# A hybrid decoder step on one core: when the decode branch's cached values are loaded, and in which buffers

## The chip, the core and the metric

The kernel runs as one program on one core of a Trainium2 chip. The metric is the device time of one execution in microseconds (us), as the median of several runs. Five engines work side by side, each through its own list of instructions in the order in which the program was recorded: PE (matmuls; PEld are its weight loads), DVE, ACT, POOL, and SP, which here only issues transfers (DMAs). An engine that waits for another holds up everything behind it on its own list.

## What is computed

Two layers of a decoder. Each layer handles 512 prompt tokens and 64 sample tokens (8 sequences of 8 tokens) with shared weights. The part that the change touches is the attention of the sample tokens over a cache of old keys and values, three head groups with window and dilation (128, 1), (512, 4) and (2048, 16):

```python
def dilated_group(q, k_all, v_all, q_idx, window, dilation):
    n_keys = window // dilation + 1
    idx = q_idx[:, None] - jnp.arange(n_keys)[None, :] * dilation
    ...
    s = jnp.einsum('bthd,btjhd->bhtj', q, kg).astype(jnp.float32) * (HEAD_DIM ** -0.5)
    ...
    m = jnp.max(s, axis=-1, keepdims=True)
    p = jnp.exp(s - m)
    den = jnp.sum(p, axis=-1, keepdims=True)
    o = jnp.einsum('bhtj,btjhd->bthd', p / den, vg.astype(jnp.float32))

def layer(x, ...):
    proj = rmsnorm(x, norm1) @ w_in            # q, k, v, u, ga, gb
    ...
    mixed = jax.nn.sigmoid(ga) * (o_a @ w_pa) + jax.nn.sigmoid(gb) * (o_b @ w_pb)
    x = x + mixed @ w_o
    x = x + jnp.square(jax.nn.relu(rmsnorm(x, norm2) @ w_up)) @ w_down
```

## The kernel before

**Stages of a layer.** PE first does the q, k, v projections in units ("d", "a", "b", "e", "c"), for two passes `p` of two heads each. Then follow the four products for `u` (weights `wu`), the gate products for branch b (`wgb`, `wpb`), those for branch a (`wga`, `wpa`), the output product (`wo`) and the feed-forward part. The prompt's attention (`prompt`) and the sample's attention (`decode`) run beside these as generators. A small planner keeps a model time per engine, and each generator yields until a moment of it or until a mark such as `("O", p)`. So the order on every engine is fixed when the program is recorded.

**The decode branch.** `decode(p, qb)` has two parts. In the first, DVE and POOL multiply nine key chunks by the queries `qb` and fold them into scores `SC`. In the second, PE multiplies the weights by nine value chunks into the PSUM tile `po`. A chunk is a tile of 128 x 8 x 128 floats, 512 KB, loaded by `chunk` on SP's queue: the 128 and 512 groups in one DMA, the 2048 group in two DMAs of half the size. All chunks live in four buffers with the tag `kc`. In the value part one chunk of the 128 group comes first, and then four steps `c`, each with a chunk of the 512 group and one of the 2048 group. After each step DVE copies the result from `po` to `at`, and PE begins the next step only after that copy. Before, four value chunks (128, 512/0, 2048/0, 512/1) are asked for together ahead of the softmax; each of the other five is asked for when a buffer has been read: the first at the mark `N`, the others through `more()` after each chunk of a step.

**The queries' tile.** `qb` holds 128 x 8 x 3 x 128 floats, filled by eight DMAs from the DRAM copy `DQ`. It has one buffer, for both passes of a layer. After the new keys' products of a pass it is read no more, and after the second pass it is not filled again in that layer.

**What stands on SP's queue near the end of the first pass.** `out_p<-nat` writes keys and values of the prompt from `nat`. After the projections the memory of `nat` is given to the tiles of the `u` stage, so DVE's first write into a `u` tile waits for these two writes. The first of them waits on SP until `DV<-nat` (issued by ACT in `turn`) has landed, because the two share one of the eight completion counters of SP's and ACT's queues. `sn` (the pooling state) stands behind them.

**Where PE is alone with decode.** At the first gate product of branch a, the main sequence stops at `until("D", 1)`: there the value part of the second pass runs on PE with no other product beside it.

Of the kernel before, what the change touches and what calls it, by code (L numbers as in the profile page):

```python
# [7 lines left out]
F32 = mybir.dt.float32  # L8
# [83 lines left out]
def hybrid_decoder_kernel(ctx: ExitStack, tc: tile.TileContext, a, o):  # L92
# [21 lines left out]
    def C(name):  # L114
        lo, hi = OFF[name]
        return const[:, lo:hi]
# [127 lines left out]
    def side(gen, delay=0.0):  # L244
        sides.append([now[0] + delay if not isinstance(delay, tuple) else delay, gen])

    def mark(*key, lat=0.0):
        ev[key] = now[0] + lat
# [137 lines left out]
    def after(*lanes, lag=0.2):  # L386
        return "at", max([now[0]] + [x.t for x in lanes]) + lag
# [158 lines left out]
    for l in range(L):  # L546
# [7 lines left out]
        dp = kvn = ve1 = None  # L554
# [307 lines left out]
        def decode_q(p, DN):  # L862
            rope(DN[:, 0:6].rearrange("p n (h d) -> p (n h) d", h=2).unsqueeze(1), *rope_d, 64, 1, 12)
            yield 1.6
            DQ = drp.tile([64, 384], F32, tag=f"dq{l}{p}", name="DQ")
            Q.dma_start(DQ, DN[:, 0:3].rearrange("p n f -> p (n f)"))
            yield 2.6
            if p == 1:
                yield ("K", 0)
            qb = dp.tile([128, 8, 3, 128], F32, tag="qb", name="qb", bufs=1)  # L870
            for b in range(8):
                Q.dma_start(qb[16 * b:16 * b + 16].rearrange("p t n f -> p (t n f)"),
                            DQ[8 * b:8 * b + 8].rearrange("t e -> (t e)").unsqueeze(0).to_broadcast([16, 3072]))
            side(decode(p, qb))
# [24 lines left out]

        def chunk(p, n, c, s):  # L900
            src = a["c" + n][l].rearrange("b r (s f) -> b r s f", s=2)[:, :, s, 128 * p:128 * p + 128]
            t = dp.tile([128, 8, 128], F32, tag="kc", name="kc", bufs=4)
            if n == "128":
                Q.dma_start(t, src.rearrange("b (g i) f -> (b g) i f", g=16))
            elif n == "512":
                Q.dma_start(t, src.rearrange("b (g i c) f -> (b g) i c f", g=16, c=4)[:, :, c])
            else:
                for i in range(2):
                    Q.dma_start(t[:, 4 * i:4 * i + 4],
                                src.rearrange("b (g i c) f -> (b g) i c f", g=16, c=16)[:, :, c + 4 * i])  # L910
            return t

        def decode(p, qb):
            todo = [("512", 0), ("2048", 0)] + [(n, c) for c in range(1, 4) for n in ("512", "2048")]
            if p == 1:
                yield ("V", 0)
            k1 = chunk(p, "128", 0, 0)
            got = [chunk(p, *todo.pop(0), 0)]
            if p == 1:
                yield ("D", 0)  # L920
            SC = dp.tile([128, 23, 8, 2], F32, tag="SC", name="SC", bufs=1)
            sq = SC.rearrange("p s t h -> p s (t h)")
            got += [chunk(p, *todo.pop(0), 0) for _ in range(2)]
            late = []

# [37 lines left out]
            sm = tp.tile([128, 3, 16], F32, tag="dsm", name="dsm", bufs=1)  # L963
            V.tensor_reduce(out=sm[:, 0], in_=sq.rearrange("p s q -> p q s"), axis=AX.X, op=ALU.max)
            todo = [("128", 0)] + [(n, c) for c in range(4) for n in ("512", "2048")]
            got = [chunk(p, *x, 1) for x in todo[:4]]
            del todo[:4]
            yield ("O", p)
            yield after(V)
            po = opp.tile([128, 512], F32, tag="o", name="po")  # L970
# [17 lines left out]
            V.tensor_mul(sq, sq, sm[:, 2].unsqueeze(1).to_broadcast([128, 23, 16]))  # L988
            yield after(V)

            def spread(s0, n, t):
                src = sq[:, s0:s0 + n] if t is None else SC[:, s0:s0 + n, t]
                q = 16 if t is None else 2
                return (src.unsqueeze(2).to_broadcast([128, n, 8, q]),
                        C("bd8").unsqueeze(1).unsqueeze(3).to_broadcast([128, n, 8, q]))

            for s0, n, vv in ((20, 3, kvn[:, 3:6]), (0, 8, got.pop(0))):
                pb = dp.tile([128, 8, 8, 16], F32, tag="prod", name="pb", bufs=3)
                V.tensor_mul(pb[:, 0:n], *spread(s0, n, None))
                yield after(V)  # L1000
                for s in range(n):
                    T.matmul(pof, vv[:, s], pb[:, s].rearrange("p b q -> p (b q)"), start=(s0 == 20 and s == 0),
                             stop=False, skip_group_check=True)
            mark("N", p)
            got.append(chunk(p, *todo.pop(0), 1))

            def more():
                if todo:
                    got.append(chunk(p, *todo.pop(0), 1))

            def pairs(c):
                pb = dp.tile([128, 8, 2, 8, 2], F32, tag="prod", name="pb2", bufs=3)
                qs = dp.tile([128, 8, 16, 2], F32, tag="pb3", name="pb3", bufs=2)
                for i in range(2):
                    t = c + 4 * i
                    V.tensor_mul(pb[:, :, i], *spread(8, 8, t))
                    V.tensor_mul(qs[:, 4 * i:4 * i + 4], SC[:, 16:20, t].unsqueeze(2).to_broadcast([128, 4, 16, 2]),
                                 C("bdz")[:, 8 - 8 * i:24 - 8 * i].unsqueeze(1).unsqueeze(3)
                                 .to_broadcast([128, 4, 16, 2]))
                return [pb[:, s].rearrange("p i b h -> p (i b h)") for s in range(8)], \  # L1020
                       [qs[:, s].rearrange("p x h -> p (x h)") for s in range(8)]
# [4 lines left out]
            for c in range(4):  # L1026
                area = po_[:, 128 + 128 * (c % 3):256 + 128 * (c % 3)]
                ws = nxt
                if c < 3:
                    nxt = pairs(c + 1)  # L1030
                for w, vv in zip(ws, (got.pop(0), got.pop(0))):
                    for s in range(8):
                        r = 32 * (s % 4)
                        T.matmul(area[r:r + 32], w[s], vv[:, s], start=False, stop=(w is ws[1] and s > 3),
                                 skip_group_check=True)
                        if s % 4 == 3:
                            yield 0.1
                    more()
                if c == 2:
                    mark("V", p)  # L1040
                V.tensor_copy(at[:, c], area)
                if c == 0:
                    V.memset(area, 0.0)
# [160 lines left out]
        for f in range(8):  # L1204
# [9 lines left out]
            t = gate.pop(0)  # L1214
# [411 lines left out]
```

## Time and profile before

| what | value |
|---|---|
| median of 3 runs | 1742.92 us (1741.65 to 1745.79) |
| the profiled execution, its own time | 1745.91 us |
| its span from first to last instruction | 1744.1 us |
| PE busy in it | 1638.9 us, 94% |
| DVE, ACT, POOL busy | 67%, 40%, 14% |
| mean granted TensorE clock | 0.96 of 2.4 GHz |

The page gives the busy time of each engine, the share of the granted clock by slices, and the waits. A granted clock of 0.50 is the lower of the two levels, 1.2 GHz. PE is busy nearly all the time, so the few stretches where it stands still, and those where it runs at the lower level, are where time can go.

### The profile page before, as it was taken

What the parts mean: (1) busy time and instruction counts of PE and PEld (TensorE: products, weight loads), DVE (VectorE), ACT (ScalarE), POOL (GpSimd) and SP (SyncE); (2) the same over time, 40 slices, a digit from 0 to 9 for tenths busy, and PEclk for the clock granted to TensorE, in tenths of its full rate; (3) what the DMA queues carried; (4) which work ended last, traced back from release to release, by engine and by line L of the source; (5) the groups of instructions that cost most, each with busy time, mean ns of one, the idle gap of its engine ahead of it and who ended that gap; (6) DMA issues with size and microseconds to landing.
All of it is one profiled execution on the core that took longest, in us unless ns stands there. A gap on an engine that the chain in (4) does not pass through costs nothing.

```text
span 1744.1 us, 30710 instructions
## 1 busy us (share of the span) xinstructions
PE 1638.9 (94%) x12608; PEld 1592.0 (91%) x12608; DVE 1166.7 (67%) x1892; ACT 695.4 (40%) x1210; POOL 239.6 (14%) x370
## 2 busy tenths in 40 slices
PE   8999879899989999999999989797998999999997
PEld 8989769889889999999998988696998999999996
DVE  5489569646766666666636966794566666766664
ACT  5544332123444343443434544221344433443444
POOL 0041023000011111111001400330000211111102
PEclk9999989989989999999999999898998999999999
DMA  4665643434235545543428475335251455445431
GB/s 174 129 205 136 171 117 109 141 92 137 100 112 192 179 165 187 192 159 103 133 81 184 144 184 152 112 100 142 78 187 44 161 176 193 171 167 176 160 100 62
DMA packets 140166, 248.93 MB, mean 143 GB/s; under 512 B 10332, under 2 KB 100956, under 8 KB 137706
## 3 DMA queue, kind: packets, MB, share of 16 engines
q1 hardware_dynamic: 132398, 187.65, 35.7%
q0 software_dynamic: 4736, 56.34, 9.1%
q10 hardware_dynamic: 2892, 2.98, 0.5%
q8 instruction: 99, 1.62, 0.4%
q14 instruction: 41, 0.34, 0.1%
HBM read 233.10 MB, written 68.58 MB: 173 GB/s over the span
## 4 chain that ended last, share of the span: by engine, by line
PE 76%; DVE 10%; DMA 6%; ACT 4%; issue 2%; SPq 0%; POOL 0%; DVEq 0%; POOLq 0%; ACTq 0%
PE mm L380 41%; PE pa L380 10%; PE mmq L380 10%; PE pc L380 5%; DMA kc<-in_c 2%; PE pb L380 2%; DVE wl L357 2%; PE po L380 2%; PE psd L380 2%; DMA DV<-nat 1%; ACT wh L357 1%; PE O L380 1%; DVE SC L357 1%; PE trx L384 1%; DVE xr L357 1%
## 5 line engine op out<-in xcount | busy, mean ns | idle before, releaser
L380 PE MATMUL mm<-m,wh 128*128 128x256 f32 (+1 forms) x2560 | 450.4, 296 | 3.4 <-DVE xr L357 2.1
L380 PEld LDWEIGHTS mm<-m,wh 128*128 128x128 f32 x2560 | 386.7, 189 | 4.4 <-ACT wh L357 1.7
L380 PE MATMUL mm<-m,wl 128*128 128x320 f32 (+1 forms) x1280 | 281.7, 297 | 8.0 <-DVE wl L357 8.0
L357 DVE TENSOR_TENSOR wl<-raw,wh 128x1024 fp32r<-128x1024 f32 (+2 forms) x195 | 220.8, 1134 | 77.1 <-ACT wh L357 73.5
L357 ACT CAST wh<-rawu 128x512 fp32r<-128x512 f32 (+1 forms) x158 | 123.1, 783 | 350.6 <-DVE rawu L357 299.9
L357 ACT CAST wh<-raw 128x1024 fp32r<-128x1024 f32 (+2 forms) x195 | 183.1, 940 | 171.2 <-PE mm L380 86.0
L380 PE MATMUL mm<-a,wh 128*128 128x256 f32 (+1 forms) x1280 | 231.4, 304 | 12.7 <-DVE ud L357 12.4
L380 PEld LDWEIGHTS mm<-m,wl 128*128 128x128 f32 x1280 | 217.6, 190 | 8.9 <-DVE wl L357 8.9
L380 PE MATMUL mmq<-wh,a 128*128 128x256 f32 x1152 | 219.0, 290 | 1.2 <-DVE a L357 0.5
L380 PEld LDWEIGHTS mm<-a,wh 128*128 128x128 f32 x1280 | 194.9, 193 | 17.0 <-issue 16.3
L380 PEld LDWEIGHTS mmq<-wh,a 128*128 128x128 f32 x1152 | 182.6, 195 | 4.3 <-issue 1.4
L357 DVE TENSOR_TENSOR xr<-xr,mm 128x576 f32<-128x576 f32 (+2 forms) x152 | 108.7, 716 | 116.0 <-PE mm L380 110.8
L357 DVE TENSOR_TENSOR wl<-rawu,wh 128x512 fp32r<-128x512 f32 (+1 forms) x158 | 140.2, 889 | 65.6 <-ACT wh L357 61.9
L380 PE MATMUL pa<-h,wh 128*128 128x288 f32 x896 | 181.7, 295 | 0.0
L357 POOL COPY pace<-beat 1x1 f32<-1x1 f32 x112 | 60.7, 542 | 867.9 <-DVE beat L357 867.9
L380 PE MATMUL mmq<-wl,a 128*128 128x256 f32 x576 | 164.8, 286 | 0.0
L380 PEld LDWEIGHTS pa<-h,wh 128*128 128x128 f32 x896 | 144.8, 188 | 0.0
L380 PE MATMUL mm<-a,wl 128*128 128x256 f32 (+1 forms) x640 | 138.7, 299 | 0.0
L380 PE MATMUL pa<-h,wl 128*128 128x288 f32 x448 | 132.4, 296 | 0.0
L380 PEld LDWEIGHTS mmq<-wl,a 128*128 128x128 f32 x576 | 112.0, 194 | 0.0
L380 PEld LDWEIGHTS mm<-a,wl 128*128 128x128 f32 x640 | 109.5, 192 | 0.0
L380 PE MATMUL pc<-h,wh 128*128 128x288 f32 x512 | 104.6, 296 | 0.0
(212 smaller groups left out, 2581.8 us busy)
## 6 DMA issues: line engine op xcount, KB each, us to landing
out_s<-in_c POOLq DMA_DIRECT2D x64, 508.0 KB, 5.0
rawu<-in_wup SPq DMA_DIRECT2D x60, 512.0 KB
raw<-in_wd SPq DMA_DIRECT2D x60, 512.0 KB
kc<-in_c SPq DMA_DIRECT2D x40, 512.0 KB
raw<-in_wq SPq DMA_DIRECT2D x35, 512.0 KB
kc<-in_c SPq DMA_DIRECT2D x64, 256.0 KB
out_s<-in_c POOLq DMA_DIRECT2D x32, 504.0 KB, 5.1
raw<-in_wgb SPq DMA_DIRECT2D x16, 512.0 KB
```

The lines of the kernel that those rows point to most:

```text
L357: return op(*args, **kw)
L380: return self.eng.matmul(out, w, x, **kw)
L384: return self.eng.transpose(out, x, one)
```

## The change

`values()` now issues the value loads as a generator of its own. The 128 chunk is still asked for at once. In the first pass (`p == 0`) the next three follow 8 us of planner time later and 3 us apart. In the second pass (`p == 1`) six more follow 0.3 us apart, the last three of them into three parts of a tile with the tag `qb`, the buffer that the queries of that pass held. The value part waits for the mark `("values", p)`, so that all of them have been recorded; `more()` asks for the rest. In the second pass that leaves two chunks (512/3 and 2048/3).

```diff
         def chunk(p, n, c, s):
             src = a["c" + n][l].rearrange("b r (s f) -> b r s f", s=2)[:, :, s, 128 * p:128 * p + 128]
-            t = dp.tile([128, 8, 128], F32, tag="kc", name="kc", bufs=4)
+            if room:
+                t = room.pop(0)
+            else:
+                t = dp.tile([128, 8, 128], F32, tag="kc", name="kc", bufs=4)
...
+        room = []
...
             todo = [("128", 0)] + [(n, c) for c in range(4) for n in ("512", "2048")]
-            got = [chunk(p, *x, 1) for x in todo[:4]]
-            del todo[:4]
+            got = [chunk(p, *todo.pop(0), 1)]
+
+            def values():
+                for i in range(3 if p == 0 else 6):
+                    if i == 3:
+                        more = dp.tile([128, 3, 8, 128], F32, tag="qb", name="kc", bufs=1)
+                        room.extend(more[:, j] for j in range(3))
+                    got.append(chunk(p, *todo.pop(0), 1))
+                    yield (3.0, 0.3)[p]
+                mark("values", p)
+
+            side(values(), 8.0 if p == 0 else 0.3)
             yield ("O", p)
...
+            yield ("values", p)
             for s0, n, vv in ((20, 3, kvn[:, 3:6]), (0, 8, got.pop(0))):
...
             mark("N", p)
-            got.append(chunk(p, *todo.pop(0), 1))
-
-            def more():
-                if todo:
-                    got.append(chunk(p, *todo.pop(0), 1))
+            more()
```

The lists of PE, DVE, ACT and POOL are the same before and after, apart from line numbers and buffer names. Only SP's list changes, at two places in each layer.

The first place is SP's list at the end of the first pass; `wgb` is the first gate weight, `kc` are value chunks (the two DMAs of a 2048 chunk are the rows of 128x4x128).

```order
-L340 DMA kc<-in_c 128x8x128 x2
-L340 DMA kc<-in_c 128x4x128 x2
-L340 DMA kc<-in_c 128x8x128
-L340 DMA qb<-DQ 16x3072 x8
-L340 DMA raw<-in_wgb 128x1024
-L340 DMA out_p<-nat 128x4x128 x2
+L340 DMA kc<-in_c 128x8x128
+L340 DMA qb<-DQ 16x3072 x8
+L340 DMA raw<-in_wgb 128x1024
+L340 DMA kc<-in_c 128x8x128
+L340 DMA out_p<-nat 128x4x128 x2
+L340 DMA kc<-in_c 128x4x128 x2
```

Ahead of the two `out_p` writes stood four chunks, and now two; the chunks 2048/0 and 512/1 follow behind them, ahead of `sn`.

The second place is SP's list in the second pass, after the first four value chunks.

```order
 L340 DMA raw<-in_wpa 128x256
-L340 DMA raw<-in_wga 128x1024
-L340 DMA kc<-in_c 128x4x128 x2
-L340 DMA kc<-in_c 128x8x128
-L340 DMA kc<-in_c 128x4x128 x2
+L340 DMA kc<-in_c 128x4x128 x2
+L340 DMA kc<-in_c 128x8x128
+L340 DMA kc<-in_c 128x4x128 x2
+L340 DMA raw<-in_wga 128x1024
 L340 DMA kc<-in_c 128x8x128
 L340 DMA kc<-in_c 128x4x128 x2
```

The weight load `wga` moved behind the five DMAs of 2048/1, 512/2 and 2048/2. Those five no longer wait for a read of a `kc` buffer by PE, since they go into the queries' tile; the last three DMAs (512/3, 2048/3) still do.

## Rows read from the trace of the kernel before

**Rows 1.** The page: its head and section 1 (busy us and share).

```profile
span 1744.1 us, 30710 instructions
PE 1638.9 (94%) x12608; PEld 1592.0 (91%) x12608; DVE 1166.7 (67%) x1892; ACT 695.4 (40%) x1210; POOL 239.6 (14%) x370
```

**Rows 2.** Timeline, PE: start us, us, engine line op [idle before <-releaser].

```profile
188.47 1.30 PE L380 MATMUL mm<-a,wh 128*128 128x256 f32 x4 [5.91 <-DVE ud L357]
...
1046.32 1.30 PE L380 MATMUL mm<-a,wh 128*128 128x256 f32 x4 [6.45 <-DVE ud L357]
```

**Rows 3.** Timeline, DVE, the first write of a u tile in layer 0.

```profile
187.50 0.69 DVE L357 TENSOR_TENSOR u<-mm,rb 128x512 f32<-128x512 f32 x1 [8.53 <-DMA out_p<-nat]
```

**Rows 4.** Timeline, SP's issues (start us, us), layer 0, then one of layer 1.

```profile
167.40 9.38 SPq L340 DMA_DIRECT2D qb<-DQ  x8
...
183.81 0.95 SPq L340 DMA_DIRECT2D out_p<-nat  x2
187.50 0.37 SPq L340 DMA_DIRECT2D sn<-in_state_pool  x1
...
1041.65 0.95 SPq L340 DMA_DIRECT2D out_p<-nat  x2
```

**Rows 5.** Timeline, ACT's issues of DV, layer 0 and layer 1.

```profile
173.46 0.37 ACTq L340 DMA_DIRECT2D DV<-nat  x1
...
1030.77 0.38 ACTq L340 DMA_DIRECT2D DV<-nat  x1
```

**Rows 6.** Waits of SP from 170 to 200 us: us in total, times, longest.

```profile
SPq L340 <- DMA DV<-nat: 5.8, 1, 5.8
```

**Rows 7.** Windows: stretch, us, busy by engine, PEclk, DMA share, GB/s.

```profile
160.00:165.00 5.00, 5.00 (x48) 4.75 (x47) 3.56 (x10) 1.15 (x6) 0.00 (x0) 1.00 0.81 233
165.00:170.00 5.00, 5.00 (x47) 4.44 (x45) 4.62 (x9) 4.95 (x16) 0.00 (x0) 1.00 1.05 282
```

**Rows 8.** Timeline, PE, value part of the second pass, layer 0.

```profile
345.62 0.43 PE L380 MATMUL po<-kc,pb 128*32 128x128 f32 x8 [0.48 <-DMA kc<-in_c]
347.70 0.66 PE L380 MATMUL po<-kc,pb 128*32 128x128 f32 x8 [1.66 <-DMA kc<-in_c]
349.58 1.51 PE L380 MATMUL po<-kc,pb 128*32 128x128 f32 x24 [1.22 <-DVE pb L357]
351.29 0.65 PE L380 MATMUL po<-kc,pb 128*32 128x128 f32 x8 [0.21 <-DMA kc<-in_c]
353.19 2.24 PE L380 MATMUL po<-kc,pb 128*32 128x128 f32 x32 [1.24 <-DMA kc<-in_c]
355.85 1.91 PE L380 MATMUL po<-const,at 128*128 128x32 f32 x8 [0.41 <-DVE at L357]
```

**Rows 9.** Waits of PE from 1190 to 1240 us, layer 1's value part.

```profile
PE po L380 <- DMA kc<-in_c: 5.9, 6, 2.2
```

**Rows 10.** Timeline, PE, value part of the second pass, layer 1.

```profile
1199.45 1.35 PE L380 MATMUL po<-kc,pb 128*32 128x128 f32 x32
...
1206.44 1.45 PE L380 MATMUL po<-kc,pb 128*32 128x128 f32 x24 [2.23 <-DMA kc<-in_c]
...
1210.05 1.50 PE L380 MATMUL po<-kc,pb 128*32 128x128 f32 x24 [1.25 <-DMA kc<-in_c]
```

**Rows 11.** Windows: after the stop of layer 0; the value part of layer 1.

```profile
188.40:193.10 4.70, 4.63 (x19) 4.67 (x20) 3.52 (x9) 2.38 (x4) 0.00 (x0) 0.50 0.44 131
...
1206.90:1215.20 8.30, 5.39 (x64) 3.22 (x57) 0.58 (x2) 0.00 (x0) 0.00 (x0) 0.50 0.45 113
```

**Rows 12.** Timeline, SP's issues in the second pass, layer 0.

```profile
333.71 0.34 SPq L340 DMA_DIRECT2D raw<-in_wga  x1
342.30 7.82 SPq L340 DMA_DIRECT2D kc<-in_c  x8
```

**Rows 13.** Timeline, layer 0: ACT's cast of that wga, and PE's first read of sn.

```profile
363.03 1.04 ACT L357 CAST wh<-raw 128x1024 fp32r<-128x1024 f32 x1
...
197.70 0.61 PE L384 MATMUL trs<-const,sn 120*128 120x120 f32 x4
```

More of the change, by code (lines that the diff above doesn't have):

```diff
@@ L989, in decode, with more @@
             yield after(V)
+            def more():
+                if todo:
+                    got.append(chunk(p, *todo.pop(0), 1))
             def spread(s0, n, t):
```

## Prediction

> **What bounds the kernel now.** I read the page's head first: PE is busy for 1638.9 of 1744.1 us [rows 1]. The change leaves the lists of PE, DVE, ACT and POOL as they are, so it can win only where PE stands still, or runs at the lower clock, because of something on SP's queue. The waits of PE by stretches show two such places per layer, and the timeline shows each one's chain.
>
> The first place is the start of the `u` stage. PE stands for 5.91 us in layer 0 and 6.45 us in layer 1 [rows 2]. DVE is named there, but DVE itself stood for 8.53 us until the `out_p` writes had landed, since the `u` tiles take over the memory of `nat` [rows 3]. These writes were issued at 183.81 [rows 4], after SP had waited 5.8 us for `DV<-nat` [rows 6], which ACT had issued at 173.46 [rows 5]. So DV took 10.35 us to land, and in layer 1 10.88 us (1030.77 to 1041.65) [rows 4, 5]. In that time SP's queue was still moving what had been issued earlier: four value chunks and eight `qb` loads, whose issues alone lasted 9.38 us from 167.40 [rows 4].
>
> The second place is the value part of the second pass, where PE has no other product to do. In layer 0 it waits before five groups of matmuls [rows 8]; in layer 1 six waits for chunks make 5.9 us [rows 9]. The eight DMAs for the last five chunks are issued only from 342.30 on, as the buffers are read [rows 12].
>
> **Part 1, first pass, loads spaced out.** In SP's list the chunks 2048/0 and 512/1 move from ahead of `qb` and `out_p` to behind them, and 512/0 to behind `qb`. Two chunks of 512 KB, 1.05 MB, are then no longer ahead of DV and `out_p`. While the chunks moved, the DMAs carried 233 and 282 GB/s [rows 7]. That makes 4.5 us or 3.7 us; I take 3.7, from the stretch in which the last chunks moved. If DV waits for what stands ahead of it, it lands 3.7 us sooner, `out_p` is issued at 180.1 in place of 183.81, and DVE's write follows by as much. PE's stops shrink from 5.91 to 2.2 and from 6.45 to 2.75 us: 7.4 us in the two layers. Something of the stop stays, because DV still has the eight `qb` loads ahead of it.
>
> The bounds: at the least nothing, if DV's time doesn't depend on those chunks; at the most the whole stop, 12.4 us. The clock comes on top. After the stop of layer 0 PE ran 4.70 us at 0.50, 1.2 GHz [rows 11], so it lost half of that, 2.35 us. A stop of 2 to 3 us may end in the same stretch or in none, so I count nothing in the sum and 2 x 2.35 us in the range; the other way, a shorter stop might let the lower clock fall on PE's work in place of its idle time, and I allow the same 2.35 us per layer as a loss.
>
> The Trainium skill, page "DMA: Bandwidth & Descriptors", section "Queues, rings and completion order", speaks against this part: an engine "round-robins between the queue rows it has work for", so a transfer on ACT's queue shares the engines with SP's queue and doesn't stand behind it. By that rule the sum of part 1 would be nothing, and the time is that of the second rival below. The trace agrees only in part: sharing equally, DV's 512 KB with as much from SP's queue would need 3.7 to 4.5 us at the rates of [rows 7], and it took 10.35 and 10.88 [rows 4, 5].
>
> What moves to behind `out_p` must still be in time. `sn` gets three more DMAs ahead of it; PE reads it at 197.70 [rows 13], 10.2 us after its issue at 187.50 [rows 4], and both move by the same amount. PE reads the value chunks of the first pass behind that in its list. The two chunks ahead of `sn` are 1.05 MB, 4.5 us at 233 GB/s [rows 7], and fit into the 10.2. If that cover were gone, PE would wait one for one.
>
> **Part 2, second pass, seven of nine chunks ahead.** The chunks 2048/1, 512/2 and 2048/2 go into the queries' tile and need no buffer that PE has to read first. They are issued right after the first four, before the 333.71 of the `wga` load [rows 12]. At 233 GB/s [rows 7] their 1.57 MB need 6.7 us, so they are there by about 341, before PE's first wait at 345.62 [rows 8].
>
> Layer 0: the waits inside the steps are 0.48, 1.66 and 0.21 us. Those at the starts of steps 2 and 3 are 1.22 and 1.24, and each holds DVE's copy of the step before, which stays. What it costs alone is the 0.41 us ahead of the last group [rows 8]. (The 1.22 is put down to DVE, but the program waits there for chunk 512/2 too.) Sum: 0.48 + 1.66 + 0.21 + 0.81 + 0.83 = 4.0 us.
>
> The two chunks that are still asked for late, 512/3 and 2048/3, take the place in SP's list of what before were the first two of the late ones. Those let PE go on at 347.70 and 349.58. Step 3, which needs them, would start at 353.19 - 4.0 = 349.2 and want 2048/3 about 1.1 us later, at half of its 2.24 us [rows 8]. So they are just in time, and I count nothing.
>
> Layer 1: 5.9 us less two copies of 0.41 is 5.1 [rows 8, 9]. Steps 2 and 3 then run 3 to 4 us sooner, mostly before 1206.90, where the clock fell in this trace [rows 11]. At the lower clock 24 matmuls took 1.45 and 1.50 us; at the higher one 32 took 1.35, so 24 take 1.01 [rows 10]. That is 0.9 us more. The second late chunk let PE go on at 1206.44 [rows 10], about 0.4 us after step 3 would now want it: 0.4 off. Layer 1: 5.6 us. The bounds of part 2: 2 us for each layer if the late two chunks still hold step 3 (as 0.83 did) and the clock falls sooner; up to 4.15 us more per layer, half of the 8.30 us at 1.2 GHz [rows 11], if the clock stays up.
>
> The `wga` load moves past five DMAs and lands some 6.7 us later, about 341 to 344. ACT casts it at 363.03 [rows 13], after this change perhaps 8 us sooner, so ten us of cover are left; without it ACT's cast would be late one for one.
>
> **The sum.** 7.4 + 4.0 + 5.6 = 17.0 us. The profiled execution took 1745.91 us, 3 us above the median of the runs; from it 1728.9, from the median 1742.92 it makes 1725.9. I predict 1725.9 for the median. Nothing I see gives the time back later: PE is busy 94% of the span [rows 1], and each load there waits for a DVE or PE instruction that moves along.
>
> **The rivals.**
>
> *Both stops go altogether.* DV finds the queue so much emptier that `out_p` lands before PE needs the `u` tiles, and PE stays at 2.4 GHz. That gives 12.4 + 2 x 2.35 = 17.1 for part 1 and 9.6 for part 2, 26.7 in all: 1716; with the clock kept up in the value part as well 1708. Against it: eight `qb` loads still stand ahead of DV. Chance 0.17.
>
> *DV lands as late as before.* Its time depends on sharing with SP's queue, not on the two chunks. Part 1 then gives nothing, part 2 gives 9.6: 1733.3. For it: the `qb` loads and the gate weight stay ahead, and 512/0 too. Against it: DV needed 10 us, more than twice what sharing explains. The Trainium skill's rule of that section would make this the outcome. Chance 0.20.
>
> *No change.* The queue is full, the same bytes move, and the waits only change their names: `out_p` is held by `qb` in place of the chunks, and the value part by the late two chunks, each taking up what the others let go. 1742.9. Against it: SP issues nothing between the `wga` at 333.71 and 342.30 [rows 12], so there is room for the three chunks. Chance 0.08.
>
> *Slower: `sn` comes late.* With chunk loads ahead of it in SP's queue, `sn` lands after PE wants it, and PE's list stops at the transposes. The eight `qb` loads, as many bytes as three chunks, took 9.38 us to issue [rows 4]. If the chunks took twice that, 18.8 us, PE would stand 18.8 - 10.2 = 8.6 us, plus 2.35 for the clock, in each layer. That is 22 us against the gain of 17: 1748. It decides from 8.5 us lost per layer (6.15 of stop, 2.35 for the clock), that is from `sn` needing over 16 us from its issue. Chance 0.05.
>
> **How the numbers follow.** My own sum has 0.50; its own range is 1718 to 1731, from 2.35 us of clock per layer and 4 us in part 2 either way. A measurement of this kernel can tell about 0.2%, 3.5 us. Faster by more than that holds the sum and the first two rivals, 0.87; same 0.08; slower 0.05. For 8 in 10 the range leaves out no change, slower, and the far end of the first rival: 1708 to 1736.
>
> **What would show it.** In the profile after: `out_p` issued 3 to 4 us sooner after DV's issue than 10.35 and 10.88 us; PE's stop before the third `u` product at 2 to 3 us; in the value part of the second pass no wait for a chunk except at step 3, and about 4 to 5 us less from its first matmul to the first gate product. I am wrong on part 1 if DV still takes 10 us or more, on part 2 if waits for chunks still make over 2 us in a layer, and on both if PE stops at the transposes of `sn`.

## The result, and the profile after

The changed kernel took 1714.42 us (median, 1712.42 to 1719.43), the kernel before 1742.29 us beside it: ratio 0.9842, interval 0.9822 to 0.9863. The forecast was 1725.9 us, with a range of 1708 to 1736: right in sign and within the range, but 11 us too slow. The same kernel, measured twice more (e0 and c1 below), gave 0.9873 and 0.9850. The mean of the three is 0.9855, some 25 us of 1742 where the sum had 17.0.

The page after, its head and PE in section 1, against [rows 1]:

```profile
span 1713.6 us, 30708 instructions
PE 1623.2 (95%) x12608; PEld 1580.0 (92%) x12608; DVE 1166.2 (68%) x1892; ACT 695.6 (41%) x1210; POOL 239.7 (14%) x370
```

The span is 30.5 us shorter, and PE is busy 15.7 us less with the same 12608 matmuls. So half of the gain is not waiting but matmuls that ran at the higher clock. The 12608 matmuls of the two profiles stand in the same order, so their start times can be compared one by one: some 24 of the 30.5 us are won at the two places of each layer, and some 6.5 elsewhere (2.7 ahead of the first place, 1.7 between the two layers' places, 2.1 behind the last). Elsewhere PE waits for no transfer in either profile, but the stretches at the lower clock make 42 us in place of 56; they fall there a little differently from profile to profile. That is why the repeats below count.

**First place.** The timeline of PE after, the two stops ahead of the third `u` product, against [rows 2]:

```profile
181.84 0.77 PE L380 MATMUL mm<-a,wh 128*128 128x256 f32 x4 [1.95 <-DVE ud L357]
...
1028.32 1.30 PE L380 MATMUL mm<-a,wh 128*128 128x256 f32 x4 [4.34 <-DVE ud L357]
```

The stops are 1.95 and 4.34 us, where they were 5.91 and 6.45. ACT's issue of DV and SP's issues in layer 0, against [rows 4, 5]:

```profile
170.79 0.37 ACTq L340 DMA_DIRECT2D DV<-nat  x1
```

```profile
157.95 7.60 SPq L340 DMA_DIRECT2D qb<-DQ  x8
167.89 0.36 SPq L340 DMA_DIRECT2D raw<-in_wgb  x1
168.29 0.56 SPq L340 DMA_DIRECT2D kc<-in_c  x1
176.97 0.95 SPq L340 DMA_DIRECT2D out_p<-nat  x2
177.96 2.05 SPq L340 DMA_DIRECT2D kc<-in_c  x3
180.93 1.74 SPq L340 DMA_DIRECT2D sn<-in_state_pool  x1
```

`out_p` is issued 6.18 us after DV (170.79 to 176.97), where it was 10.35; in layer 1 it is 8.68 us, where it was 10.88. The two moved chunks follow it. PE reads `sn` at 188.99 us, 8 us after its issue, without a wait.

The DMA engines in slices of 0.625 us from 165 us on, after (first busy share in tenths, then GB/s):

```profile
DMA  9979997978979999970029999999999999981678
GB/s 157 197 138 197 177 197 118 164 125 164 184 198 351 314 299 327 374 243 18 0 88 288 238 173 282 347 297 342 342 302 290 297 317 277 328 315 66 105 203 341
```

The two zeros are 176.25 to 177.5 us: DV has landed only when nothing is left to move, and the engines stand empty until `out_p` starts. The first eight slices, in which the `qb` loads move, run at 118 to 197 GB/s with the engines nearly fully busy, and the next four, mostly the gate weight `wgb`, at 125 to 198; the chunk and DV behind them run at 299 to 374.

What moved while DV was on its way can be told from the packets, since each load has its own packet size here: 12 KB for `qb`, 4 KB for `wgb`, 512 bytes for a chunk, 1 KB for DV; q1 is SP's queue and q10 ACT's. From DV's issue to `out_p`, layer 0, before (173.46 to 183.79 us) and after (170.79 to 176.95):

```profile
DMA packets 845, 2.00 MB, mean 193 GB/s; under 512 B 123, under 2 KB 641, under 8 KB 768
q1 hardware_dynamic: 316, 1.46, 65.3%
q10 hardware_dynamic: 528, 0.52, 17.4%
...
DMA packets 1703, 1.52 MB, mean 247 GB/s; under 512 B 56, under 2 KB 1592, under 8 KB 1701
q1 hardware_dynamic: 1174, 0.98, 63.0%
q10 hardware_dynamic: 528, 0.52, 25.1%
```

Before, 77 of the packets are of 12 KB (845 less 768): 0.95 MB of `qb`. The 127 of 4 KB are 0.52 MB of `wgb`, and the 518 of 512 bytes to 1 KB are nearly all DV's own 512. The four chunks had been moved by then; they cost time by holding up the `qb` loads behind them. After, two packets of `qb` are left (1703 less 1701); the 0.98 MB of q1 are `wgb` and chunk 512/0. Of the 6.16 us after, the first 2.96 (170.79 to 173.75) show this line alone:

```profile
q1 hardware_dynamic: 675, 0.74, 97.9%
```

So no packet of DV moved in them, while three quarters of what stood ahead in SP's queue did; all 528 of q10 fall into the other 3.2 us. In the first pass, where little else moves, DV's first packet follows its issue by 0.9 us.

**Second place.** PE in the value part of the second pass, layer 0 and then layer 1, against [rows 8 to 10]:

```profile
335.65 1.08 PE L380 MATMUL po<-kc,pb 128*32 128x128 f32 x32 [0.41 <-DVE at L357]
338.38 1.20 PE L380 MATMUL po<-kc,pb 128*32 128x128 f32 x24 [1.64 <-DMA kc<-in_c]
339.97 0.42 PE L380 MATMUL po<-kc,pb 128*32 128x128 f32 x8 [0.40 <-DMA kc<-in_c]
...
1184.02 1.08 PE L380 MATMUL po<-kc,pb 128*32 128x128 f32 x32 [0.41 <-DVE at L357]
1185.51 1.07 PE L380 MATMUL po<-kc,pb 128*32 128x128 f32 x24 [0.41 <-DVE at L357]
1186.97 0.43 PE L380 MATMUL po<-kc,pb 128*32 128x128 f32 x8 [0.40 <-DMA kc<-in_c]
```

Only step 3, with the two late chunks, still waits for a chunk: 2.04 us in layer 0, 0.40 in layer 1. DVE's copies of 0.41 us now show where chunk waits covered them.

What the clock did there is seen best in windows over the same 196 matmuls in each kernel, from the first of the value part to the eighth group of products behind it. Columns: stretch, us, busy by PE, PEld, DVE, ACT, POOL, granted clock, DMA share, GB/s. Before, layer 0 and layer 1:

```profile
338.23:363.99 25.76, 19.57 (x197) 15.73 (x196) 9.21 (x29) 3.06 (x6) 0.00 (x0) 0.67 0.41 108
1195.68:1223.30 27.62, 20.37 (x198) 16.62 (x196) 9.99 (x30) 3.13 (x6) 0.00 (x0) 0.69 0.37 101
```

After:

```profile
329.49:349.78 20.29, 16.41 (x197) 14.52 (x196) 9.81 (x30) 3.13 (x6) 0.00 (x0) 0.83 0.46 126
1178.30:1194.89 16.59, 13.88 (x197) 11.73 (x196) 9.28 (x30) 3.13 (x6) 0.00 (x0) 1.00 0.43 124
```

The two stretches together went from 53.38 to 36.88 us. PE's busy time in them fell from 39.94 to 30.29 us, and its idle time from 13.44 to 6.59. So more came from the clock (9.65 us) than from the waits (6.85 us).

### The profile page after: what moved, and what is told of

Read it like the earlier page. It is cut to its first block, busy times and chain, and to the rows that moved or that the text cites. A ratio compares the mean times of both kernels' runs of the same rounds, so it can differ in the third digit from the quotient of the medians.

```text
span 1713.6 us, 30708 instructions
## 1 busy us (share of the span) xinstructions
PE 1623.2 (95%) x12608; PEld 1580.0 (92%) x12608; DVE 1166.2 (68%) x1892; ACT 695.6 (41%) x1210; POOL 239.7 (14%) x370
## 4 chain that ended last, share of the span: by engine, by line
PE 77%; DVE 11%; DMA 5%; ACT 4%; issue 2%; SPq 0%; POOL 0%; POOLq 0%; DVEq 0%; ACTq 0%
PE mm L380 42%; PE pa L380 10%; PE mmq L380 10%; PE pc L380 5%; PE pb L380 2%; DVE wl L357 2%; DMA kc<-in_c 2%; PE psd L380 2%; PE po L380 2%; ACT wh L357 1%; PE O L380 1%; DVE SC L357 1%; PE trx L384 1%; DMA DV<-nat 1%; DVE xr L357 1%
## 5 line engine op out<-in xcount | busy, mean ns | idle before, releaser
L380 PEld LDWEIGHTS mm<-a,wh 128*128 128x128 f32 x1280 | 193.4, 192 | 11.3 <-issue 10.2
```

Of the source, the lines that this page charges most:

```text
L380: return self.eng.matmul(out, w, x, **kw)
```

## The experiments

My theory: two gains that don't need each other, part 1 by what stands ahead in SP's queue, part 2 by waits and the clock that they pull down. Rivals are named with each run. Each ratio is to runs of the kernel before beside it.

**The changed kernel again (e0, c1).** No edit.

> The changed kernel once more, beside the kernels it is compared with. All theories: 0.984 of the kernel before, about 1714 to 1716 us. If the places of the lower TensorE clock are set by the program, PE runs at 0.50 in the same stretches as in its first profile (340.3 to 347.1, 1026.3 to 1033.2, nothing between 1105 and 1306 us); if they fall by chance, they stand elsewhere, and the share of the gain that I put down to the clock in the value part of layer 1 (5 to 6 us) is one trace's luck.

> The changed kernel a third time, beside the next one. 1714 to 1720; stops before the third u product between 1.9 and 6.4 us in each layer.

e0: 1719.36 us, ratio 0.9873 (0.9858 to 0.9889). c1: 1717.21 us, 0.9850 (0.9830 to 0.9871). Stops: 4.00 and 4.56 in e0, 1.98 and 3.72 in c1. The two value stretches take 34.40 and 35.81 us together. So the value part repeats: in e0 too no stretch at 0.50 lies in that of layer 1. Elsewhere the stretches at 0.50 moved, and e0's time is above what I expected. The first stop does not repeat: 1.95 us was a good one.

**One part alone (e1, e2).** e1 keeps the spacing of the first pass:

```diff
-            side(values(), 8.0 if p == 0 else 0.3)
+            if p == 0:
+                side(values(), 8.0)
+            else:
+                got += [chunk(p, *todo.pop(0), 1) for _ in range(3)]
+                mark("values", p)
```

e2 is the same with `p == 1` and 0.3: the second pass alone.

> Only the first pass is spaced out; the second pass asks for four chunks at once and for the rest through the buffers, as before. Theory (two gains that add up): 8 us less than the kernel before, 1734; stops before the third u product of 1.95 and 4.34 us as in the changed kernel, value parts of the second pass with waits for chunks of 4 to 6 us in each layer as before. Rival (the gains aren't additive: each place moves the lower clock of the other): 3 us or 12 us less, 1739 or 1730, with the stops as said and the lower clock at other places.

> Only the second pass loads seven of nine ahead; the first pass asks for four chunks at once as before. Theory: 17 us less than the kernel before, 1725; out_p 10 to 11 us behind DV and stops of 5.9 and 6.4 us as before, waits for chunks in the value parts of about 2 us in layer 0 and 0.4 in layer 1. Rival (of the 17, the 7 above the waits came only because part 1 moved the lower clock): 10 us less, 1732, with the lower clock inside the value part of layer 1 as before.

e1: 0.9974 (0.9963 to 0.9986), 4.5 us less than before. e2: 0.9895 (0.9876 to 0.9914), 18.3 us less. Together 22.8, within the uncertainty the 25 us of the whole change: the gains add up. The rivals (1739 or 1730 for e1; 1732 for e2) rest on the clock moving between the places. By its time e2's rival is out, and e1's 1736.95 us lies between; the windows of the value stretches in e2, then in e1, speak against both:

```profile
336.07:353.88 17.81, 15.20 (x196) 13.32 (x196) 9.19 (x30) 3.14 (x6) 0.00 (x0) 0.90 0.49 137
1185.49:1201.93 16.44, 13.72 (x197) 11.73 (x196) 9.28 (x30) 3.13 (x6) 0.00 (x0) 1.00 0.44 128
```

```profile
332.97:359.75 26.78, 20.69 (x197) 16.97 (x196) 10.35 (x30) 3.12 (x6) 0.00 (x0) 0.68 0.39 104
1191.70:1217.42 25.72, 18.86 (x197) 15.41 (x196) 9.99 (x30) 3.13 (x6) 0.00 (x0) 0.73 0.40 108
```

e2 has 34.25 us with the clock up, e1 has 52.50 with it down, whatever the first pass does. PE's stops in e2, then in e1:

```profile
186.90 1.30 PE L380 MATMUL mm<-a,wh 128*128 128x256 f32 x4 [8.22 <-DVE ud L357]
...
1035.89 1.30 PE L380 MATMUL mm<-a,wh 128*128 128x256 f32 x4 [8.50 <-DVE ud L357]
```

```profile
183.76 1.30 PE L380 MATMUL mm<-a,wh 128*128 128x256 f32 x4 [5.20 <-DVE ud L357]
...
1041.78 1.30 PE L380 MATMUL mm<-a,wh 128*128 128x256 f32 x4 [4.20 <-DVE ud L357]
```

e1's stop in layer 0 is 5.20 us, not the 1.95 that I expected. e2's stops are longer than those of before with the same first pass, against my 5.9 and 6.4. In that profile PE came there earlier, but `out_p` could not: it was issued 12.66 us after DV (169.57 to 182.23). The stop takes up what PE gains ahead of it.

**Less ahead of DV (e7, twice).** 512/0 goes behind `out_p` too; the other engines' lists stay.

```diff
-            side(values(), 8.0 if p == 0 else 0.3)
+            side(values(), 10.0 if p == 0 else 0.3)
```

> The changed kernel with 512/0 behind out_p too, so that one value chunk of the first pass stands ahead of DV in place of two (four before the change). Theory (what stands ahead in SP's queue sets when DV has landed): 0.52 MB less ahead, 1.9 us at 282 GB/s, off each of the two stops before the third u product, which in the changed kernel's profiles so far were 1.95 to 6.37 us; 3.7 us less than the changed kernel, 1714 to 1716. Rival (the qb loads alone set DV's landing, and chunks add nothing): stops and time of the changed kernel, 1719.

> 512/0 behind out_p too, a second time, on the chip of the changed kernel. Theory (out_p's first write is no longer the eighth transfer behind DV, goes out 9 us before the second, and less stands ahead of both): stops of 0 to 1 us in both layers, 4 to 7 us less than the changed kernel of this call. Rival (the first profile was lucky): stops between 2 and 6 us and the same time.

1712.46 us, 0.9826 (0.9808 to 0.9844), and 1713.55 us, 0.9832 (0.9811 to 0.9853); beside the second the changed kernel had 1717.21. That is about 4 us better, the best version of this study, though the ranges of the runs touch. PE's stops, in both profiles:

```profile
179.78 0.77 PE L380 MATMUL mm<-a,wh 128*128 128x256 f32 x4 [0.71 <-DVE ud L357]
...
1023.95 0.77 PE L380 MATMUL mm<-a,wh 128*128 128x256 f32 x4 [1.66 <-DVE ud L357]
```

```profile
183.06 0.77 PE L380 MATMUL mm<-a,wh 128*128 128x256 f32 x4 [2.63 <-DVE ud L357]
...
1024.19 1.30 PE L380 MATMUL mm<-a,wh 128*128 128x256 f32 x4 [3.15 <-DVE ud L357]
```

The stops in layer 0 and layer 1 of all profiles whose transfers near DV differ only in the chunks ahead of it (so without e3, e4, e5 and e8):

| chunks ahead of DV | kernels | stops, us | mean |
|---|---|---|---|
| four | before, e2 | 5.91, 8.22 and 6.45, 8.50 | 7.07 and 7.48 |
| two | after, e0, c1, e1, e6, e11 | 1.95, 4.00, 1.98, 5.20, 6.37, 5.53 and 4.34, 4.56, 3.72, 4.20, 1.98, 3.63 | 4.17 and 3.74 |
| one | e7, e7b | 0.71, 2.63 and 1.66, 3.15 | 1.67 and 2.41 |

Two chunks are worth 2.9 and 3.7 us, one more 2.5 and 1.3. That is near the 1.9 us per chunk that I read from the DMA rate. Single stops scatter by 4 us, and the second e7 did not repeat the first one's near zero. e7 also has another change in it: one transfer fewer lies between DV and `out_p`, so its first write no longer waits for DV. So the step from two chunks to one is not the price of a chunk alone. The step has a limit: in e7's profile `sn` came late for the first time, in layer 0 by 0.86 us, and in layer 1 PE waited 1.77 us before the same matmul, which the profile puts down to a `wgb` load; in the second e7 it waited in neither:

```profile
187.94 0.60 PE L384 MATMUL trs<-const,sn 120*128 120x120 f32 x4 [0.86 <-DMA sn<-in_state_pool]
...
1033.02 1.03 PE L384 MATMUL trs<-const,sn 120*128 120x120 f32 x4 [1.77 <-DMA raw<-in_wgb]
```

**The shared counter (e3, e4, e8).** A small load more on SP's queue moves the turn of the counters on by one, in the changed kernel (e3) and in the kernel before (e4):

```diff
+    shim = cp.tile([1, 8], F32, name="shim")
...
+            if p == 1:
+                Q.dma_start(shim, a["gains"][0:1, 0:8])
             side(decode(p, qb))
```

> The changed kernel with one 32-byte load more on SP's queue behind the qb loads of the second pass. It moves the turn of the eight completion counters on by one, so that out_p waits for a qb load in place of DV. Theory (queue order: out_p would still have the qb loads, wgb and 512/0 ahead of it on SP's queue, so only the gap goes in which SP waits while nothing is left to move): out_p issued 2 to 5 us sooner, its data there 2 to 3 us sooner, stops 2 to 3 us shorter in each layer, 4 to 6 us less than the changed kernel, 1714. Rival (the shared counter alone makes the stop): out_p issued at once behind 512/0, no stop in either layer, 9 us or more less, 1710 or below. Second rival (counters don't matter): 1719, stops as in the changed kernel.

> The kernel before with the same 32-byte load and so the same shift of the counters: four chunks stand ahead of out_p, but out_p no longer waits for DV. Theory (queue order): stops of 5.9 to 8.5 us become 3 to 6, 4 to 6 us less than before, 1736, about what spacing out the first pass alone gave. Rival (the shared counter alone): no stop, 12 to 14 us less, 1728.

e3: 1719.22 us, 0.9865 (0.9849 to 0.9882), as the changed kernel; e4: 1.0011 (0.9995 to 1.0028), as the kernel before. e3's time is that of the rival in which counters don't matter, and e4's is that of no expectation; but neither run tests them, for the edit did less than I thought. The eighth transfer recorded after DV waits for it, and with one more in between that is the one just ahead of `out_p`: the chunk 512/0 in e3, `wgb` in e4. SP's issues in e4:

```profile
174.69 0.23 SPq L340 DMA_DIRECT2D shim<-in_gains  x1
179.64 0.36 SPq L340 DMA_DIRECT2D raw<-in_wgb  x1
180.04 0.98 SPq L340 DMA_DIRECT2D out_p<-nat  x2
186.98 0.36 SPq L340 DMA_DIRECT2D sn<-in_state_pool  x1
```

`out_p` stands in SP's list behind the waiting `wgb`, so it goes out at 180.04, with `wgb`'s 512 KB issued just ahead of it, and takes until 186.98. The stops were 7.91 and 9.33 us, in e3 5.74 and 6.87.

e8 takes DV off these counters: the kernel before, with DV issued on POOL's queue.

```diff
-            S.dma_start(DV.rearrange("(j p) f -> p j f", j=4), nat)
+            G.dma_start(DV.rearrange("(j p) f -> p j f", j=4), nat)
```

> The kernel before with DV issued on POOL's queue, which has completion counters of its own; POOL stood idle there for 39 us. Nothing else moves, and no load or write on SP's queue waits for DV any more. Theory (the u tiles wait for the writes out of nat, and these for all that is ahead in the queue, four chunks and eight qb loads): out_p issued 3 to 5 us sooner, but landing only 2 to 4 us sooner; stops of 6 to 8 us become 3 to 6, 4 to 7 us less than before, 1737. Rival (the shared counter alone makes the stop): no stop, 12 to 14 us less, 1729. Second rival (DV shares packet by packet and itself holds the u tiles, landing as late as ever): stops and time as before, 1742.

0.9982 (0.9968 to 0.9997), 3.2 us less than before. The edit also brings DV's issue forward, against what I wrote: POOL, which stood idle, issues it at 166.40 us, where ACT had come to it at 173.46. Its stops, and `out_p`'s issue with DVE's first write of a `u` tile in layer 0:

```profile
184.93 1.17 PE L380 MATMUL mm<-a,wh 128*128 128x256 f32 x4 [3.67 <-DVE ud L357]
...
1039.69 1.30 PE L380 MATMUL mm<-a,wh 128*128 128x256 f32 x4 [4.03 <-DVE ud L357]
...
174.71 1.63 SPq L340 DMA_DIRECT2D out_p<-nat  x2
...
183.96 0.69 DVE L357 TENSOR_TENSOR u<-mm,rb 128x512 f32<-128x512 f32 x1 [6.30 <-DMA out_p<-nat]
```

`out_p` was issued 9 us sooner than before, yet the `u` tiles were free only 3.5 us sooner, of which 1.3 had been won ahead of this place. The counter alone (no stop, 1729) is out: with it gone, and DV issued sooner, over half of the stop stays, and the trace names `out_p` for it, with the queue ahead of it. My theory's 4 to 7 us were a little too many. The interval of the time ends near 1, so that DV itself holds the tiles as late as ever (1742) is out by the trace alone: DV landed 14.5 us after its issue, at 180.9, and in layer 1 at 1036.0, 3 us ahead of DVE's write in both.

**DV in larger rows (e5).** DV is written in 4 KB rows and read back to match:

```diff
-            S.dma_start(DV.rearrange("(j p) f -> p j f", j=4), nat)
+            S.dma_start(DV.rearrange("(p j) f -> p j f", j=4), nat)
...
-            G.dma_start(vcs[p], DV.rearrange("(n r) f -> n r f", r=4))
+            for j in range(4):
+                G.dma_start(vcs[p][32 * j:32 * j + 32],
+                            DV.rearrange("(a r j) f -> j a r f", r=4, j=4)[j])
```

> The changed kernel with DV written in rows of 4 KB in place of 1 KB (read back in four loads on POOL's queue so that the same values arrive); out_p still waits for DV. Theory (DV shares the DMA engines packet by packet with the 12 KB packets of qb, so its 512 small packets need as many turns): with a quarter of the packets DV lands 2 to 4 us sooner than the 6.2 to 10.6 us of the changed kernel's profiles, stops of 0 to 3 us, 4 to 7 us less than the changed kernel, 1713 to 1715. Rival (DV lands when SP's queue has drained, whatever its packets): 6 to 10 us and 1719.

0.9835 (0.9818 to 0.9852), stops of 3.10 and 3.11 us, `out_p` 7.5 us behind DV in both layers. The time lies in my theory's range (1713 to 1715), but the delays lie among those of the changed kernel (6.2 to 10.6 us), and the interval overlaps with two of the changed kernel's three (not with e0's). No run of the changed kernel stands beside it. Whether the size of DV's packets matters stays open.

**The chunks of the second pass (e11, e6).** e11 has five of nine ahead in place of seven (one in the queries' tile):

```diff
-                for i in range(3 if p == 0 else 6):
+                for i in range(3 if p == 0 else 4):
...
-                        room.extend(more[:, j] for j in range(3))
+                        room.append(more[:, 0])
```

e6 doesn't load the last two at all; the last step reads chunks that are there already.

> The changed kernel with five of the nine chunks of the second pass ahead in place of seven (one in the queries' tile); 512/2 and 2048/2 are asked for late too. Theory (the value part costs its waits and, once PE has stood several times, a long stretch at 0.50 behind them): waits for chunks of 2 to 4 us in each layer in place of 0.3 to 2, and the stretch of 13.7 us at 0.50 back in one layer at least; 6 to 14 us more than the changed kernel. Rival (the clock has nothing to do with the chunks): the waits alone, 3 to 5 us more. Second rival (two late chunks or four are the same, since each has its buffer in time): no difference.

> The changed kernel without the loads of chunks 512/3 and 2048/3 in the second pass; the last step reads chunks that are there already, so that part of the result is left wrong. Theory (what is left of waits in the value part is the two late chunks): the waits of 1.64 and 0.40 us in layer 0 and 0.40 in layer 1 go, 2.4 us less than the changed kernel, 1712. Rival (behind the chunk stands DVE, which writes the step's weights and the copies): the same waits stay under the name of DVE, and the time is that of the changed kernel within 1 us.

e11: 0.9948 (0.9930 to 0.9965), 17 us more than the changed kernel beside it (1734.30 to 1717.21), above what I expected. e6: 0.9869 (0.9849 to 0.9889), the changed kernel's time. The value stretches in e11, then in e6:

```profile
336.33:359.05 22.72, 17.31 (x196) 14.46 (x196) 9.39 (x30) 3.14 (x6) 0.00 (x0) 0.77 0.37 101
1187.55:1212.34 24.79, 19.20 (x198) 16.37 (x196) 9.93 (x30) 3.13 (x6) 0.00 (x0) 0.72 0.33 91
```

```profile
337.21:352.90 15.69, 13.37 (x196) 11.76 (x196) 9.20 (x30) 3.13 (x6) 0.00 (x0) 1.00 0.30 87
1180.23:1196.00 15.77, 13.46 (x197) 11.85 (x196) 9.27 (x30) 3.13 (x6) 0.00 (x0) 1.00 0.21 63
```

Two chunks fewer ahead cost 11.7 us in the two stretches (47.51 against c1's 35.81): PE stands 5.6 us longer and is busy 6.1 us longer, at a clock of 0.77 and 0.72. The rival without the clock allowed 3 to 5 us. Behind the waits the clock fell for 10.2 us in each layer, where I had expected 13.7. The rest of the 17 us does not lie in the value part: in these two profiles most of it is the stop of layer 0, 5.53 us against c1's 1.98, which the edit doesn't touch. In e6 the stretches are 2.9 us below those of e0, which ran beside it (31.46 against 34.40), with the clock up throughout, about as my theory said, but the whole time is not. The stops don't explain that: 6.37 and 1.98 us make about as much as e0's 4.00 and 4.56. Compared matmul by matmul, e6's profile loses 4.6 us to e0's at places that neither edit touches. So the rival's number came true and its reason did not: DVE did not take over the waits.

## Why the prediction came out as it did

**Part 1: right.** The step was: two chunks less ahead of DV, 3.7 us each layer off the stops, 7.4 in all. The stops fell by 2.9 and 3.7 us on average, 6.6 in all; e1's time gave 4.5 (2.4 to 6.4). The DMA rate was about the right price for a chunk, and the reason held too: after the change, in layer 0, DV's packets moved behind nearly all that stood ahead in SP's queue (none in the first 2.96 us). What was wrong is the list of what still moved beside DV. I named four value chunks; before, these had been moved when DV was issued, and 0.95 MB of `qb` and 0.52 MB of `wgb` were left. Two chunks fewer ahead let the queue come to its end sooner all the same. And what DV still had ahead of it after the change were not the eight `qb` loads, as I wrote, but `wgb` and chunk 512/0, which the `qb` loads had held up: of `qb` itself two packets were left in layer 0.

The rival "DV lands as late as before" fell with e1 and e7. The Trainium skill's rule behind it (page "DMA: Bandwidth & Descriptors", section "Queues, rings and completion order", taking turns between queues) would give e1 nothing; e1 measured 0.9974, with an interval below 1. That does not refute the rule: with turns, DV can still end last and the chunks still delay it. The trace agrees in part: before, 492 of q10's 528 packets moved from 173.46 to 179.0, beside 0.76 MB of q1's; after, q10 moved nothing in its first 2.96 us. Why it differs stays open.

"Both stops go altogether" held neither in the changed kernel nor, on its second profile, in e7. "`sn` comes late" cost nothing here; e7, one chunk further, showed it begin. My sign of being wrong on part 1, DV at 10 us or more, came once in the profiles with two chunks ahead (10.6 us, layer 0 of e6).

**Part 2: the mechanism right, the clock mis-sized.** My sum had 9.6 us: 8.7 of waits and 0.9 of clock. Over the four profiles with four chunks ahead (before, e1, e4, e8) the two value stretches make 52.42 us on average, over eight with seven ahead (after, e0, c1, e2, e3, e5, e7, e7b) 35.07. That is 17.35 us: 7.5 less idle, 9.8 less busy. The waits were sized well. The clock was not, and it is nearly the whole miss of the forecast.

The step that failed stands in two sentences of the prediction. In layer 0 I counted no clock at all, and in layer 1 only the two steps that "run 3 to 4 us sooner, mostly before 1206.90, where the clock fell". I took the fall as fixed in time and moved the work ahead of it. But the waits themselves bring the fall: with five chunks ahead it lasts 10.2 us, with nothing late (e6) it does not come. Before, the long stretches at the lower clock were these:

```profile
346.70:360.36 13.66, 9.49 (x92) 6.96 (x93) 3.21 (x11) 1.50 (x4) 0.00 (x0) 0.50 0.56 146
1206.90:1220.56 13.66, 10.75 (x86) 8.58 (x79) 3.63 (x8) 1.83 (x5) 0.00 (x0) 0.50 0.31 79
```

In each layer 13.66 us at 0.50 (1.2 GHz) begin among the waits, with 20.25 us of PE work in both. At 2.4 GHz it takes half, so 10.1 us were to be had, which agrees with the 9.8. I had read the clock for 8.30 us of layer 1 alone [rows 11], and put "if the clock stays up" in the range, as the far end of a rival, where it was the likely case. A smaller slip: the row of 1.35 us that I took for 32 matmuls at the higher clock [rows 10] lies half at the lower, which ended at 1200.1; after, 32 take 1.08. That makes my 0.9 us of clock 1.3. A stretch of 13.7 us stands there in each profile with four chunks ahead, in both layers; with seven ahead the granted clock over the whole value stretch is 0.83 to 1.00.

No single wait for a chunk was above 2.3 us before [rows 8 to 10], and each long stretch at 0.50 began among several of them. How few are enough stays open: in layer 0 of the first profile after, 6.8 us at 0.50 follow waits of 1.64 and 0.40 us. The Trainium skill tells of the like on its page "TensorE: Matmul & The Clock Gate", section "A second HAM failure mode: psum-queue depth-cycling", in a kernel that cycles through PSUM banks: many small idle times between groups of matmuls make the clock swing. The trace agrees: in the windows of before above, granted clocks of 0.67 and 0.69 go with 6.2 and 7.3 us of idle time, in waits of 0.2 to 2.2 us.

The late two chunks were "just in time" as forecast: 0.3 to 0.5 us of waits in most layers of the eight profiles, up to 1.15 in some. In layer 0 of the first it was 2.04, just over the 2 us that I had named as a sign of being wrong on part 2.

## What to carry to other kernels

Where PE works alone and waits for several loads in a row, price the whole stretch at the lower clock that begins among the waits, not the waits alone: here it was more than half of what that place gained. An access that frees memory, like `out_p`, is held by all that its queue has been given earlier, and by any transfer that its completion counter has to wait for; so ask for what is needed late only behind it, and look up which waiting transfer stands ahead of it on the issuing engine. One profile of a stop that ends with a DMA scatters by some us, so compare several.

## What was unexpected of the hardware

The eight `qb` loads (192 KB each) run at 118 to 197 GB/s with the DMA engines nearly fully busy, and the gate weight right behind them no faster, where the chunk and DV that follow reach 299 to 374. Why they are slow was not tried. DV's 512 KB took 6.2 to 10.6 us until `out_p` could go with two chunks ahead, and 10.35 to 12.91 with four (8.7 and 10.2 in e4, where the gate weight stood behind DV). And a transfer can be held by a counter that it shares with an unrelated one eight transfers earlier: moving that wait by one transfer gained nothing, since `out_p` stands behind the waiting transfer in SP's list.
